# Seven blocks of the first feed-forward input and the attention's output with both operand parts in one 512-column matmul, and new tables of order

## The chip, the cores and the metric

The kernel runs on one core of one Trainium2 chip. The metric is the device time of one execution in microseconds. Five engines work side by side: TensorE (PE, with its weight loads listed as PEld), VectorE (DVE), ScalarE (ACT), GpSimd (POOL) and SyncE (SP), which here issues the transfers of weights.

## The reference, cut to what matters

Two layers at sequence 256 and width 1024, in float32. The feed-forward width is 2816, that is 22 blocks of 128.

```
mods = silu(c) @ ada_w + ada_b                   # shift, scale, gate, four sets; one more pair for kv
x = x + gate * hgrn2_mixer(modulate(x, ...))     # layer 0: gated linear recurrence
x = x + gate * swiglu(modulate(x, ...), w_in, w_out)
x = x + gate * nsa_mixer(modulate(x, ...), w_q, w_out, shared kv)   # layer 1: sparse attention
x = x + gate * swiglu(modulate(x, ...), w_in, w_out)
swiglu(h) = (silu(a) * b) @ w_out,  a, b = split(h @ w_in)
```

## The kernel before

**Products.** Each float32 product is made of reduced-precision parts. A weight chunk of 1 MB lands in one of four `raw` buffers; it has two halves of 128x1024, and each half is split into a high part `wh` (a cast on ACT, L321) and the rest `wl` (a subtraction on DVE, L325). The activations are split into `hh` and `hl` likewise. A narrow product, `mm3` (L535 to L537), is three matmuls of 256 columns for each 128 rows of the inner dimension (a k-step): wh with hh, wh with hl, wl with hh, all summed in one PSUM tile. A wide product, `gemm_wide` (L547, L548), lays hh and hl beside each other: one matmul of 512 columns with wh, and one of 256 with wl. The part from hl then stands in a half of its own and must be added: in a feed-forward block by a copy on ACT (L1197) and an addition on DVE (L1198).

**Stages.** In the profiled execution: start and the first projections to 62.6 us; the recurrence ("hgrn") to about 166; the first feed-forward input ("f0", blocks `ff_0` to `ff_21`; the first three are deferred, that is computed before the norm is known and scaled by it behind, L791) to 296.2; its output (`ffo`) to 358; the keys, values, queries and softmax of the attention ("nsa") to 507; the attention's output `nso`, eight halves of eight k-steps, to 533, the first block of the second feed-forward within it; the second feed-forward input ("f1") to 656 and its output to the end. All blocks of f1 but the deferred ones are wide, all else is narrow. A feed-forward block has two halves, the gate `a` and the value `b`; behind them stand the silu `fs` (ACT L469), the product `fg` (DVE L1188 in a deferred block, L1206 in a narrow one, L1200 in a wide one) and the split of it into `g` (ACT L530, DVE L531).

**Modulation.** The vectors from `c` need 1 MB chunks of `ada_w`. Some are reduced on DVE (L390, two per chunk), some on PE (`adapsg`, `adapsss`, L429).

**Order.** All weight chunks form one list, `SCHED`, which SP issues in that order through the four raw buffers; a buffer is given back when its chunk has been split or reduced. Each engine works through a fixed list of instructions. The tables `ORDER` set the order of chunks and steps: `hgrn` and `nsa` name projections and steps; `hada`, `f0` and `f1` say before which block a modulation chunk is taken. `PRI` gives offsets of priority to a scheduler that lays the steps of all engines side by side. `QACT` and `KACT` are bit masks that say for which of eight pieces of q's and kv's input ACT forms the scaled part instead of DVE. `residual` adds a finished piece of an output to x on DVE (L800), then forms the next layer's operand (L586 on ACT, L587 on DVE) and the sum of squares.

## Time and profile before

| | |
|---|---|
| time, three runs | 723.38, 720.93, 723.20 us; median 723.2 |
| profiled execution, its own time | 723.27 us |
| its span | 721.5 us, granted clock 0.998 |

By stage (us of busy time):

| stretch | length | PE | DVE | ACT |
|---|---|---|---|---|
| hgrn 62.6 to 166 | 103.4 | 102.58 | 79.78 | 76.63 |
| f0 in, narrow blocks, 187.8 to 296.2 | 108.4 | 108.40 | 98.99 | 53.60 |
| f0 out 296.2 to 358 | 61.8 | 61.80 | 50.73 | 28.11 |
| kv, q, softmax 358 to 507 | 149.0 | 146.52 | 125.10 | 94.35 |
| nso 507 to 533 | 26.0 | 26.00 | 19.31 | 15.96 |
| f1 in 533 to 656 | 123.0 | 122.78 | 100.28 | 74.23 |

A PE that reads as busy is one with a matmul in it; successive matmuls overlap, so the time that a matmul costs is read from the distance between starts. Idle time of an engine is given with what ended it, in square brackets behind a row or behind the second bar of a group.

### The profile page before, as it was taken

The page shows a single profiled execution, that of the slowest core. Times are in us where ns is not written, and L with a number is a line of the kernel's source. Part 1 is how long each engine was busy: PE and PEld are TensorE (multiplying, and loading weights), DVE is VectorE, ACT ScalarE, POOL GpSimd, SP SyncE. Part 2 cuts the span into 40 slices and gives each one's busy share as a digit, 9 for nine tenths or more (in the row PEclk, how much of TensorE's full clock was granted, in tenths as well). Part 3 has the DMA queues.
Part 4 walks back from the last instruction along what each step waited for, and adds up shares of the span by engine and source line. Part 5 has one row for each costly group of instructions (what it writes and reads, how often), then busy time and mean ns, then how long its engine had stood idle before and what let it go on. Part 6 is the DMA issues. An engine that isn't in the chain of part 4 may idle for free.

```text
span 721.5 us, 14615 instructions
## 1 busy us (share of the span) xinstructions
PE 710.4 (98%) x5843; PEld 628.2 (87%) x5843; DVE 578.9 (80%) x1177; ACT 418.5 (58%) x825; POOL 12.3 (2%) x29
## 2 busy tenths in 40 slices
PE   8999999999999999999999999999999999999998
PEld 5999788899999999988898896555999888888887
DVE  6997896589998989889598798878779878776651
ACT  5659877567636454544376555559657656564430
POOL 0000000000000000000002020100000000000000
PEclk9999999999999999999999999999999999999999
DMA  9899865734599898888548542674445757556720
GB/s 356 334 367 381 334 255 194 269 126 175 179 343 369 315 347 341 318 304 341 198 148 289 207 151 70 248 281 187 176 175 177 256 204 258 202 197 232 241 81 23
DMA packets 27926, 174.05 MB, mean 241 GB/s; under 512 B 3281, under 2 KB 4689, under 8 KB 8018
## 3 DMA queue, kind: packets, MB, share of 16 engines
q1 hardware_dynamic: 26656, 170.80, 64.3%
q0 software_dynamic: 768, 1.57, 0.8%
q8 instruction: 46, 0.75, 0.4%
q10 hardware_dynamic: 434, 0.74, 0.3%
q14 instruction: 22, 0.18, 0.1%
HBM read 170.48 MB, written 1.05 MB: 238 GB/s over the span
## 4 chain that ended last, share of the span: by engine, by line
PE 80%; DVE 7%; ACT 6%; DMA 4%; issue 2%; SPq 0%; ACTq 0%; DVEq 0%
PE ffo L547 11%; PE ff L535 7%; PE ff L537 7%; PE ff L536 6%; PE ffo L548 5%; PE ff L547 5%; DMA raw<-in_w 3%; PE ff L548 2%; PE po L1616 2%; PE adapsss L429 2%; DVE wl L325 2%; ACT wh L321 2%; PE ptt L1598 2%; PE s L1558 2%; ACT Pt L469 1%
## 5 line engine op out<-in xcount | busy, mean ns | idle before, releaser
L321 ACT CAST wh<-raw 128x1024 fp32r<-128x1024 f32 x199 | 206.8, 1049 | 164.0 <-PE ffo L547 43.8
L325 DVE TENSOR_TENSOR wl<-raw,wh 128x1024 fp32r<-128x1024 f32 x199 | 241.2, 1220 | 71.0 <-ACT wh L321 70.9
L547 PE MATMUL ffo<-g,wh 128*128 128x512 f32 x330 | 116.0, 394 | 0.0
L536 PE MATMUL ff<-hl,wh 128*128 128x256 f32 (+1 forms) x352 | 99.1, 282 | 0.0
L537 PE MATMUL ff<-hh,wl 128*128 128x256 f32 (+1 forms) x352 | 99.1, 282 | 0.0
L535 PE MATMUL ff<-hh,wh 128*128 128x256 f32 (+1 forms) x352 | 98.9, 282 | 0.0
L548 PE MATMUL ffo<-g,wl 128*128 128x256 f32 x330 | 93.0, 282 | 0.0
L390 DVE CUSTOM_DVE_ANT_0 junk<-raw,crep 128x1024 f32<-128x1024 f32 x64 | 77.9, 1217 | 3.1 <-DMA raw<-in_w 3.1
L547 PEld LDWEIGHTS ffo<-g,wh 128*128 128x128 f32 x330 | 62.0, 188 | 14.5
L535 PEld LDWEIGHTS ff<-hh,wh 128*128 128x128 f32 x352 | 66.3, 189 | 0.3 <-ACT hh L586 0.2
L537 PEld LDWEIGHTS ff<-hh,wl 128*128 128x128 f32 x352 | 66.5, 189 | 0.0
L536 PEld LDWEIGHTS ff<-hl,wh 128*128 128x128 f32 x352 | 66.4, 189 | 0.0
L548 PEld LDWEIGHTS ffo<-g,wl 128*128 128x128 f32 x330 | 62.0, 188 | 0.0
L547 PE MATMUL ff<-h,wh 128*128 128x512 f32 x152 | 54.1, 394 | 0.0
L548 PE MATMUL ff<-h,wl 128*128 128x256 f32 x152 | 42.6, 281 | 0.0
L469 ACT ACTIVATE Pt<-Pt,nm 128x128 f32<-128x128 f32 x64 | 28.1, 441 | 16.9 <-DVE nm L1567 16.9
L547 PEld LDWEIGHTS ff<-h,wh 128*128 128x128 f32 x152 | 28.7, 189 | 6.6
L548 PEld LDWEIGHTS ff<-h,wl 128*128 128x128 f32 x152 | 28.7, 189 | 0.0
L800 DVE SCALAR_TENSOR_TENSOR x<-ffo,mod,x 128x256 f32<-128x256 f32 x31 | 14.9, 481 | 16.5 <-PE ffo L548 11.5
L530 ACT CAST g<-fg 128x256 fp32r<-128x256 f32 x44 | 17.8, 404 | 17.4 <-DVE fg L1206 16.3
L1563 DVE CUSTOM_DVE_ANT_0 Pt<-s,cst 128x128 f32<-128x128 f32 (+1 forms) x64 | 18.9, 352 | 2.1 <-PE s L1558 2.0
L1042 DVE TENSOR_TENSOR rf<-rf 128x512 f32<-128x512 f32 x28 | 18.3, 685 | 2.2 <-ACT X L1039 1.0
(497 smaller groups left out, 1755.3 us busy)
## 6 DMA issues: line engine op xcount, KB each, us to landing
raw<-in_w SPq DMA_DIRECT2D x153, 1024.0 KB, 5.5
raw<-in_w SPq DMA_DIRECT2D x11, 512.0 KB, 6.9
w1late<-in_w SPq DMA_DIRECT2D x2, 1024.0 KB, 8.7
x<-in_x SPq DMA_DIRECT2D x2, 512.0 KB, 4.7
usq<-huq POOLq DMA_DIRECT2D x16, 64.0 KB, 2.9
out<-x SPq DMA_DIRECT2D x8, 128.0 KB, 1.9
cst<-in_cst ACTq DMA_DIRECT2D x1, 558.0 KB
usk<-huk POOLq DMA_DIRECT2D x8, 64.0 KB, 5.8
```

The costliest lines, as they stand in the source:

```text
L321: r = nc.scalar.copy(wh, u)
L325: r = nc.vector.tensor_tensor(wl, u, wh.bitcast(F32), op=ALU.subtract)
L390: r = nc.vector.tensor_tensor_reduce(out=junk, in0=t[:, h * D:(h + 1) * D], in1=self.crep, scale=1.0, scalar=0.0, op0=ALU.mult, op1=ALU.ad ...
L469: r = nc.scalar.activation(out, in_, func, **kw)
L530: self.nc.scalar.copy(hi, v)
L535: mm(ps, lhsT=wh, rhs=hh, start=first, stop=False)
L536: mm(ps, lhsT=wh, rhs=hl, start=False, stop=False)
L537: return mm(ps, lhsT=wl, rhs=hh, start=False, stop=last)
L547: mm(ps, lhsT=w[k][0], rhs=b, start=k == 0, stop=False)
L548: mm(ps[:, 0], lhsT=w[k][1], rhs=b[:, 0], start=False, stop=k == n - 1)
L1042: nc.vector.tensor_tensor(fr, fr, ap(rf, 2 * W, [1, 2], [2, n], [0, b]), op=ALU.mult)
L1563: nc.vector.tensor_tensor_reduce(out=Pt[half][:, br, o:o + n], in0=ps[half][:, br], in1=cs[:, S - n:], scale=1.0, scalar=-3e38, op0=ALU.ad ...
```

## The change

Blocks 4, 11, 14, 16, 17, 18 and 21 of f0 become wide; for that the operand `h1` is one tile with both parts beside each other. Each half of `nso` becomes wide with a PSUM tile of its own, and `residual` adds its two parts to x with two L800 in place of one. No chunk is added or taken away. The tables of order get other entries (of `hgrn` and `f0` the diff shows the lines; `hada`, `nsa` and `f1` change likewise), so do PRI and the two masks. PTV leaves the choice of engine in its line as it was. Many lines have a number higher by one in the changed kernel.

```diff
-WIDE = (1,)
+WIDE = ((4, 11, 14, 16, 17, 18, 21), range(NF))
-QACT, KACT = 0x0F, 0xF0
+QACT, KACT = 89, 241
+PTV = 1
-PRI = {"gates": -100, "av": 10, "res": 60, "rot": -15, "fh": 60}
+PRI = {'gates': -80, 'av': 10, 'res': 50, 'rot': 0, 'fh': 130}
     "hgrn": (
-        "D0 k i0 +g0 +i1 +g1 S0/4 x c0 c1 D1 i2 +i3 V0 +g2 +T0 S1/4 +g3 x G0 V1 T1 o0 H o1 G1 o2 o3"
+        "i0 k +i1 +g0 D0 +g1 S0/4 c0 x i2 c1 V0 +g2 +i3 +T0 D1 S1/4 +g3 x H G0 V1 o0 T1 G1 o1 o2 o3"
-    "f0": [7, 7, 8, 8, 9, 13, 15, 16, 16, 16, 21, 21, 22, 23, 25, 26, 28, 29, 31, 32],
+    "f0": [5, 6, 7, 8, 9, 10, 12, 13, 15, 19, 20, 20, 22, 23, 26, 26, 26, 27, 30, 32],
...
-        hh = self.hp.tile([P, KD, 258], F32R, tag=f"hh{which}", name=f"hh{which}")
-        hl = self.hp.tile([P, KD, 258], F32R, tag=f"hl{which}", name=f"hl{which}")
-        return hh, hl
+        self.h1 = self.hp.tile([P, 2, KD, 258], F32R, tag="h1", name="h1").rearrange("p e k s -> p k e s")
+        return self.h1[:, :, 0], self.h1[:, :, 1]
...
-                elif l in WIDE:
+                elif j in WIDE[l]:
+                    both = (self.h1, self.h0)[l]
...
-                        self.gemm_wide(ps[m], self.tiles(ws[m]), lambda k: self.h0[:, k, :, :S])
+                        self.gemm_wide(ps[m], self.tiles(ws[m]), lambda k: both[:, k, :, :S])
...
-                ps = self.acc_tile(f"nso{i}")
                 for m in range(2):
-                    self.gemm(ps[:, m], self.tiles(ws[m]), self.O[0], self.O[1])
-                    self.residual(ps[:, m], 2 * i + m, gate, nxt)
+                    ps = self.acc_tile(f"nso{i}_{m}")
+                    self.gemm_wide(ps, self.tiles(ws[m]), lambda k: self.h0[:, k, :, :S])
+                    self.residual(ps[:, 0], 2 * i + m, gate, nxt, ps[:, 1])
...
-                if half == 0 and br == 0:
+                if PTV >> (2 * br + half) & 1:
```

PE loses 176 matmuls, one for each wide k-step: 7 blocks of 16, and 64 in nso. Three places show the new order.

DVE at the end of the deferred blocks of f0. Before (`ISA` is the reduction L390; `u<-ff_2` are the two scaled halves of block 2; `wl_0` and `wl_1` here are the weights of blocks 5, then 6):

```order
L791 TENSOR_TENSOR u<-ff_2_0_2639,rstd 128x256
L791 TENSOR_TENSOR u<-ff_2_1_2666,rstd 128x256
L325 TENSOR_TENSOR wl_0_2698<-raw_2445,wh_0_2697 128x1024
L1188 SCALAR_TENSOR_TENSOR fg<-u,sw,fs 128x256
L325 TENSOR_TENSOR wl_1_2702<-raw_2445,wh_1_2701 128x1024
L531 TENSOR_TENSOR g<-fg,g 128x256
L1206 TENSOR_TENSOR fg<-ff_3_2709,fs 128x256
L325 TENSOR_TENSOR wl_0_2763<-raw_2455,wh_0_2762 128x1024
L531 TENSOR_TENSOR g<-fg,g 128x256
L325 TENSOR_TENSOR wl_1_2767<-raw_2455,wh_1_2766 128x1024
L1206 TENSOR_TENSOR fg<-ff_4_2774,fs 128x256
L390 ISA junk,mod_1940<-raw_2561,crep 128x1024
```

The same engine and place in the changed kernel; the wl here are those of block 5:

```order
L791 TENSOR_TENSOR u<-ff_2_0_2635,rstd 128x256
L791 TENSOR_TENSOR u<-ff_2_1_2662,rstd 128x256
L391 ISA junk,mod_2054<-raw_2442,crep 128x1024
L391 ISA mod_2054 128x1
L1188 SCALAR_TENSOR_TENSOR fg<-u,sw,fs 128x256
L391 ISA junk,mod_2054<-raw_2442,crep 128x1024
L391 ISA mod_2054 128x1
L532 TENSOR_TENSOR g<-fg,g 128x256
L414 TENSOR_TENSOR mod_2054<-mod_2054,cols 128x2
L326 TENSOR_TENSOR wl_0_2701<-raw_2452,wh_0_2700 128x1024
L326 TENSOR_TENSOR wl_1_2705<-raw_2452,wh_1_2704 128x1024
L1207 TENSOR_TENSOR fg<-ff_3_2712,fs 128x256
```

A modulation chunk (two ISA with their accumulator reads and L414) now stands between block 2 and the weights of block 5, and in the same way one before each of blocks 6 to 10; before, the first came after the weights of block 6.

PE at the end of nso. Before (`ff_0_0` and `ff_0_1` are the two halves of f1's block 0):

```order
L537 MATMUL ff_0_0_6796<-hh_6428,wl_0_6662 128x258
L535 MATMUL ff_0_0_6796<-hh_6428,wh_0_6661 128x258
L536 MATMUL ff_0_0_6796<-hl_6429,wh_0_6661 128x258
L537 MATMUL ff_0_0_6796<-hh_6428,wl_0_6662 128x258
L535 MATMUL ff_0_1_6823<-hh_6428,wh_1_6665 128x258
L536 MATMUL ff_0_1_6823<-hl_6429,wh_1_6665 128x258
L537 MATMUL ff_0_1_6823<-hh_6428,wl_1_6666 128x258
L535 MATMUL nso_6671<-h_5782,wh_1_6592 128x256
L536 MATMUL nso_6671<-h_5782,wh_1_6592 128x256
L537 MATMUL nso_6671<-h_5782,wl_1_6593 128x256
L535 MATMUL nso_6671<-h_5782,wh_1_6592 128x256
```

After:

```order
L548 MATMUL nso_1_6581<-h_5707,wh_1_6490 128x512
L549 MATMUL nso_1_6581<-h_5707,wl_1_6491 128x256
L548 MATMUL nso_1_6581<-h_5707,wh_1_6490 128x512
L549 MATMUL nso_1_6581<-h_5707,wl_1_6491 128x256
L548 MATMUL nso_1_6581<-h_5707,wh_1_6490 128x512
L549 MATMUL nso_1_6581<-h_5707,wl_1_6491 128x256
L536 MATMUL ff_0_0_6668<-h_6353,wh_0_6546 128x258
L537 MATMUL ff_0_0_6668<-h_6353,wh_0_6546 128x258
L538 MATMUL ff_0_0_6668<-h_6353,wl_0_6547 128x258
L536 MATMUL ff_0_0_6668<-h_6353,wh_0_6546 128x258
```

The last piece of nso stood behind 21 matmuls of ff_0; now nso is finished first, in pairs of 512 and 256 columns, and ff_0 follows in one piece.

DVE in the recurrence, where the decays (`rf`, L1029 to L1044) begin. Before (`wl_0_871` belongs to the projection hg_g):

```order
L1029 TENSOR_TENSOR rf_770<-rf_770,q 128x512
L1029 TENSOR_TENSOR rf_778<-rf_778,q 128x512
L1042 TENSOR_TENSOR rf_770<-rf_770 128x2x256
L1042 TENSOR_TENSOR rf_778<-rf_778 128x2x256
L1044 TENSOR_TENSOR rf_770<-rf_770 128x256
L1044 TENSOR_TENSOR rf_778<-rf_778 128x256
L1042 TENSOR_TENSOR rf_770<-rf_770 128x2x128x2
L1042 TENSOR_TENSOR rf_778<-rf_778 128x2x128x2
L1044 TENSOR_TENSOR rf_770<-rf_770 128x128
L1044 TENSOR_TENSOR rf_778<-rf_778 128x128
L325 TENSOR_TENSOR wl_0_871<-raw_704,wh_0_870 128x1024
```

After (`wl_0_821` and `wl_1_825` are both halves of the second hg_i, which now comes next on PE):

```order
L1029 TENSOR_TENSOR rf_768<-rf_768,q 128x512
L1029 TENSOR_TENSOR rf_776<-rf_776,q 128x512
L326 TENSOR_TENSOR wl_0_821<-raw_765,wh_0_820 128x1024
L326 TENSOR_TENSOR wl_1_825<-raw_765,wh_1_824 128x1024
L1042 TENSOR_TENSOR rf_768<-rf_768 128x2x256
L1042 TENSOR_TENSOR rf_776<-rf_776 128x2x256
L1044 TENSOR_TENSOR rf_768<-rf_768 128x256
L1044 TENSOR_TENSOR rf_776<-rf_776 128x256
L1042 TENSOR_TENSOR rf_768<-rf_768 128x2x128x2
L1042 TENSOR_TENSOR rf_776<-rf_776 128x2x128x2
L1044 TENSOR_TENSOR rf_768<-rf_768 128x128
```

The two subtractions for the projection that PE takes next have moved ahead of the first decay level.

## Rows read from the trace of the kernel before

**Rows 1.** The page: busy time of each engine with its share of the span and instructions; and shares of the chain that ended last.

```profile
PE 710.4 (98%) x5843; PEld 628.2 (87%) x5843; DVE 578.9 (80%) x1177; ACT 418.5 (58%) x825; POOL 12.3 (2%) x29
...
PE 80%; DVE 7%; ACT 6%; DMA 4%; issue 2%; SPq 0%; ACTq 0%; DVEq 0%
```

**Rows 2.** Busy time by stretch. Columns: stretch, its length, then PE, PEld, DVE, ACT, POOL with counts, granted clock, DMA share, GB/s.

```profile
187.80:296.20 108.40, 108.40 (x915) 108.40 (x914) 98.99 (x174) 53.60 (x81) 0.00 (x0) 1.00 0.86 325
358.00:507.00 149.00, 146.52 (x1132) 112.53 (x1131) 125.10 (x362) 94.35 (x270) 12.05 (x25) 0.99 0.56 197
507.00:533.00 26.00, 26.00 (x214) 25.51 (x213) 19.31 (x34) 15.96 (x26) 0.00 (x0) 1.00 0.53 193
```

**Rows 3.** Timeline of PE in block 5 of f0 (narrow). Columns here and in all timelines: start, duration, engine, line, operation.

```profile
205.30 0.28 PE L535 MATMUL ff<-hh,wh 128*128 128x256 f32 x1
...
207.43 0.28 PE L535 MATMUL ff<-hh,wh 128*128 128x256 f32 x1
```

**Rows 4.** Timeline of PE in block 12 of f1 (wide): the second half's first k-step, and the start of the next block.

```profile
602.90 0.39 PE L547 MATMUL ff_12b<-h,wh 128*128 128x512 f32 x1
603.13 0.28 PE L548 MATMUL ff_12b<-h,wl 128*128 128x256 f32 x1
...
605.68 0.40 PE L547 MATMUL ff<-h,wh 128*128 128x512 f32 x1
```

**Rows 5.** The page's costliest groups: count, then busy us and mean ns of one.

```profile
L547 PE MATMUL ff<-h,wh 128*128 128x512 f32 x152 | 54.1, 394 | 0.0
L548 PE MATMUL ff<-h,wl 128*128 128x256 f32 x152 | 42.6, 281 | 0.0
```

**Rows 6.** Timeline of ACT at the ends of blocks 4 and 5 of f0: the silu `fs` that waits for the end of each, and a cast that waited for its chunk.

```profile
199.50 0.38 ACT L469 ACTIVATE fs<-ff 128x256 f32<-128x256 f32 x1 [1.65 <-PE ff L537]
...
201.68 2.00 ACT L321 CAST wh<-raw 128x1024 fp32r<-128x1024 f32 x2 [0.90 <-DMA raw<-in_w]
205.20 0.39 ACT L469 ACTIVATE fs<-ff 128x256 f32<-128x256 f32 x1 [1.52 <-PE ff L537]
```

**Rows 7.** Timeline of DVE in blocks 3 to 5 of f0.

```profile
193.20 0.75 DVE L791 TENSOR_TENSOR u<-ff,rstd 128x256 f32<-128x256 f32 x2
...
195.11 0.48 DVE L1188 SCALAR_TENSOR_TENSOR fg<-u,sw,fs 128x256 f32<-128x256 f32 x1
195.51 1.22 DVE L325 TENSOR_TENSOR wl<-raw,wh 128x1024 fp32r<-128x1024 f32 x1
196.65 0.42 DVE L531 TENSOR_TENSOR g<-fg,g 128x256 fp32r<-128x256 f32 x1
196.99 0.42 DVE L1206 TENSOR_TENSOR fg<-ff,fs 128x256 f32<-128x256 f32 x1
...
200.26 1.21 DVE L390 CUSTOM_DVE_ANT_0 junk<-raw,crep 128x1024 f32<-128x1024 f32 x1
...
201.40 0.42 DVE L531 TENSOR_TENSOR g<-fg,g 128x256 fp32r<-128x256 f32 x1
...
204.02 0.15 DVE L413 TENSOR_TENSOR mod<-mod,cols 128x2 f32<-128x2 f32 x1
```

**Rows 8.** Timeline of DVE in f1: the two additions of a wide block.

```profile
558.75 0.41 DVE L1198 TENSOR_TENSOR u<-ff,u 128x256 f32<-128x256 f32 x1
559.08 0.41 DVE L1198 TENSOR_TENSOR u<-ff_3b,u 128x256 f32<-128x256 f32 x1
```

**Rows 9.** Groups of DVE in the stretch 507 to 533 (nso): the addition to x.

```profile
L800 DVE SCALAR_TENSOR_TENSOR x<-nso,mod,x 128x256 f32<-128x256 f32 x7 | 3.4, 481 | 3.5 <-PE nso L537 3.5
```

**Rows 10.** Timeline of DVE in the recurrence.

```profile
69.00 1.30 DVE L1042 TENSOR_TENSOR rf<-rf 128x512 f32<-128x512 f32 x2 [0.62 <-ACT q L1036]
...
72.53 1.21 DVE L325 TENSOR_TENSOR wl<-raw,wh 128x1024 fp32r<-128x1024 f32 x1
```

**Rows 11.** Timeline of PE at the same place.

```profile
73.80 0.39 PE L537 MATMUL hg_g<-h,wl 128*128 128x256 f32 x1 [0.63 <-DVE wl L325]
```

**Rows 12.** Timeline of DVE in the kv stage, ahead of the first weights of the attention's gates.

```profile
385.70 0.74 DVE L762 TENSOR_SCALAR t<-xr,modAkv,modkv 128x256 f32<-128x256 f32 x2
...
387.01 1.22 DVE L325 TENSOR_TENSOR wl<-raw,wh 128x1024 fp32r<-128x1024 f32 x1
```

**Rows 13.** The chain that ended last, in order of time: the transfer that follows.

```profile
388.30 9.40 DMA raw<-in_w
```

**Rows 14.** Timeline of ACT: the cast that waited for it.

```profile
397.71 1.05 ACT L321 CAST wh<-raw 128x1024 fp32r<-128x1024 f32 x1 [5.81 <-DMA raw<-in_w]
```

**Rows 15.** Timeline of PE behind that cast.

```profile
399.12 0.39 PE L988 MATMUL v<-wh,h 128*128 128x256 f32 x1 [0.43 <-ACT h L530]
...
400.74 0.39 PE L990 MATMUL v<-wh,h 128*128 128x256 f32 x1 [1.00 <-DVE h L531]
...
401.08 0.41 PE L989 MATMUL v<-wl,h 128*128 128x256 f32 x1
...
404.28 0.38 PE L535 MATMUL nq<-hh,wh 128*128 128x256 f32 x1
```

**Rows 16.** Two stretches, that of the transfer and 1 us behind PE's waits; columns as in Rows 2.

```profile
388.30:397.70 9.40, 9.40 (x85) 8.65 (x84) 5.36 (x9) 3.21 (x5) 0.00 (x0) 1.00 1.00 371
402.00:403.00 1.00, 1.00 (x6) 1.00 (x6) 1.00 (x1) 0.13 (x1) 0.00 (x0) 0.50 0.86 360
```

**Rows 17.** What PE waited for from 405 to 507 us, the longest: total, times, longest.

```profile
PE ptt L1598 <- ACT hsqq L1246: 0.2, 1, 0.2
```

More of the change, by code (lines that the diff above doesn't have):

```diff
@@ L65 @@
     "hgrn": (
-        "D0 k i0 +g0 +i1 +g1 S0/4 x c0 c1 D1 i2 +i3 V0 +g2 +T0 S1/4 +g3 x G0 V1 T1 o0 H o1 G1 o2 o3"
+        "i0 k +i1 +g0 D0 +g1 S0/4 c0 x i2 c1 V0 +g2 +i3 +T0 D1 S1/4 +g3 x H G0 V1 o0 T1 G1 o1 o2 o3"
     ).split(),
-    "hada": [1, 1, 2, 2, 3, 3, 4, 4, 7, 7, 8, 8],
-    "f0": [7, 7, 8, 8, 9, 13, 15, 16, 16, 16, 21, 21, 22, 23, 25, 26, 28, 29, 31, 32],
+    "hada": [1, 1, 1, 2, 3, 3, 4, 6, 7, 7, 9, 9],
+    "f0": [5, 6, 7, 8, 9, 10, 12, 13, 15, 19, 20, 20, 22, 23, 26, 26, 26, 27, 30, 32],
     "nsa": (
-        "K q0 c0 c1 G w0 q1 R n0 x0 q3 w1 s0 s1 s2 q2 v0 v1 n1 a s3 a s4 v2 a v3 a x1 s5 s6 v4 v6 s7 a a a a v5 a v7 a a a"
+        "q0 K c1 c0 G w0 q1 R n0 q3 q2 x0 s0 w1 s1 s2 v0 v1 n1 s3 s4 v2 a a v3 a a x1 s5 a s6 v4 v6 s7 v5 a a v7 a a a a a"
     ).split(),
-    "f1": [15, 16, 24, 29],
+    "f1": [10, 20, 21, 32],
 }
@@ L651, in startup @@
         x, v = self.x, nc.vector
-        sq = self.hp.tile([P, KD * 258], F32, tag="hh1", name="sqs")[:, :KD * S].rearrange("p (k s) -> p k s", k=KD)
+        two = self.hp.tile([P, 2, KD, 258], F32, tag="h1", name="sqs_xr0")
+        sq, self.xr0 = two[:, 0, :, :S], two[:, 1, :, :S]
         mean = self.tp.tile([P, 2, P], F32, tag="dg", bufs=1, name="mean")[:, 0]
@@ L710, in first_stat @@
         self.first_order = on_act + [A, sh], on_dve
-        self.xr0 = self.hp.tile([P, KD * 258], F32, tag="hl1", name="xr0")[:, :KD * S].rearrange("p (k s) -> p k s", k=KD)
     def stat_end(self, ps=None):
@@ L846, in hgrn @@
             v = [gp.tile([P, 2, 512], F32, tag=f"v{i}", name=f"v{i}") for i in range(2)]
-            s0 = self.hp.tile([P, KD * 258], F32, tag="hh1", name="s0")
-            s1 = self.hp.tile([P, KD * 258], F32, tag="hl1", name="s1")
+            two = self.hp.tile([P, 2, KD * 258], F32, tag="h1", name="s01")
+            s0, s1 = two[:, 0], two[:, 1]
             graw = s0[:, 1024:2048].rearrange("p (n m s) -> p n m s", n=2, m=2)
```

## The prediction

> **What bounds the kernel now.** I read the page first. PE is busy 98% of the span and holds 80% of the chain that ended last, DVE 7%, DMA 4% [rows 1]. Then the busy time by stretch: in the narrow blocks of f0 PE is busy for all of 108.40 us, in nso for all of 26.00; only the kv, query and softmax stretch leaves it 149.00 − 146.52 = 2.48 us idle [rows 2]. So a change gains in two ways: fewer or shorter PE steps, or one of the few waits of PE. The share of DVE matters too: 98.99 of 108.40 us in f0 leaves it 9.4 us, and all its work there feeds PE.
>
> The third view is the timeline of PE. Durations mislead here. By the groups a 512-column matmul lasts 394 ns and a 256-column one 281 [rows 5], so three narrow ones would be 843 ns, a wide pair 675, and a k-step would save 168. But they overlap, and the distance of starts is the price. Narrow: 205.30 to 207.43 is six k-steps, 0.355 us each, 2.84 for a half of eight; the block, from one silu's end of wait to the next, 199.50 to 205.20, is 5.70, or 2.85 a half [rows 3, 6]. Wide: 602.90 to 605.68 is a half of eight, 2.78 us [rows 4]. A half saves 0.06 to 0.07 us, not 1.3.
>
> **The change part by part.**
>
> *Wide products.* Seven blocks are 14 halves, nso is 8: 22 halves by 0.06 to 0.07 is 1.3 to 1.5 us, all on PE in stretches where it never waits. I take **−1.4**: 0.9 in f0, 0.5 in nso.
>
> The start of the 256-column matmul stands 0.23 us behind that of the 512-column one (602.90, 603.13) [rows 4]. The Trainium skill (TensorE: Matmul & The Clock Gate, Back-to-back issue gap) gives N/2.4 GHz plus about 2.5 ns from start to start, which is 216 ns for 512 columns and 109 for 256. By that rule a wide pair saves one time 2.5 ns per k-step, an estimate of 176 × 2.5 ns = 0.4 us in place of 1.4. The rows are slower than the rule for both, and they decide the sum.
>
> *What the wide blocks cost elsewhere.* Two additions on DVE per block, 0.33 us from start to start [rows 8], 0.7 a block, 4.6 to 4.9 us for seven. The idle 9.4 us of DVE in f0 [rows 2] shrink to 4.5 to 4.8, so on the whole there is cover; whether there is at each place, the next paragraph counts. In nso a second addition to x per half, 0.48 us by [rows 9], 8 × 0.48 = 3.8, in 26.00 − 19.31 = 6.7 us of idle DVE [rows 2]. PE does not wait for the pieces of nso until block 0 of f1 needs them: behind the last matmul of nso stand all the ff_0 matmuls, and the next norm's product comes after 34 of them, some 4 us at 0.12 us each, against about 2.1 us of DVE and ACT work behind the last half (two additions, an operand's two parts, a sum). Price 0; without that cover up to 2 us.
>
> *Modulation chunks earlier in f0.* This is where DVE has least to spare. The instructions of the deferred blocks ahead of the shown rows of the order are the same in both kernels but for their sequence, so the second `u<-ff_2` ends where it does now, at 193.20 + 0.67 = 193.87 [rows 7] (start to start a pair takes some 0.08 less than its 0.75). From there the new order has a reduction (1.14, from 200.26 to 201.40), fg (0.40), a reduction (1.14), g (0.34), the addition of L413 (at most 0.15) and wl of block 5 (1.14, from 195.51 to 196.65) [rows 7]: 193.87 + 4.31 = 198.2. Block 5 starts on PE at about 199.2 (the silu of block 4 starts at 199.50, when that block's last matmul, 0.28 long, has ended [rows 3, 6]), and 0.1 sooner with block 4 wide. Lead: 0.9 to 1.0 us, where the same subtraction is now done before the fg of 195.11 [rows 7], some 4.1 ahead. Carried on by the same prices (1.14 wl, 1.14 reduction, 0.34 fg, 0.34 g), block 6 has 1.4 us and block 7, behind the additions of block 4, about 1.0; blocks 8 to 10 gain 0.3 each, because DVE then needs 5.4 us a block and PE 5.70. Later blocks have more. Price **0**, with 1 us to spare; what it costs when that is used up is the second rival.
>
> *Recurrence.* PE waits 0.63 us for wl of hg_g at 73.80 [rows 11]. DVE does that subtraction at 72.53, behind two levels of decays that began at 69.00 [rows 10]. In the new order PE takes hg_i there and DVE does both its subtractions ahead of the decays, 69.00 + 1.14 = 70.1, over 2 us before PE asks. The following weights come two levels later, but PE then has a block of about 5.7 us to do. **−0.6**, between 0 (another wait of the same size behind the decays, which end 2.3 us later) and −0.63.
>
> *kv stage.* PE waits 0.43 us for h at 399.12 and 1.00 at 400.74 [rows 15]. The cause lies before: ACT's cast waited 5.81 us for its chunk [rows 14], whose transfer was issued at 388.30 and took 9.40 us [rows 13], and the h that PE needs are queued behind that cast and its subtraction. The buffer was given back by the wl of 387.01. In the new order two products L762 and one L1258 no longer stand ahead of it, as much as lies between 385.70 and 387.01 [rows 12], so the issue can come 1.3 us sooner. The DMA engines are full while it is under way (share 1.00 from 388.30 to 397.70) [rows 16], so the landing moves less than the issue. Between 0 and −1.3; I take **−0.5**, nearer to 0 because of the full queues.
>
> *Order of the queries and the softmax.* q3 and q2 now come before the first scores. The trace has only one wait left that this could remove, 0.2 us for the squares of q [rows 17], and of the 2.48 us idle of the stretch 1.43 is the kv wait; the rest, 1.05, is the most that can be had. The bound above is a new wait of the size of the largest here, 1.00 [rows 15]. I take **−0.5**, halfway to the bound: the squares leave the softmax's ACT, but no longer wait of PE goes.
>
> *The rest* (hada, f1, PRI, masks): the f1 positions fall where DVE has 123.0 − 100.28 us, as the table of stages shows. Price 0.
>
> **Sum**, against the profiled execution's own 723.27 us, which lies 0.07 above the median of the runs: −1.4 − 0.6 − 0.5 − 0.5 = −3.0, **720.3 us**. With every term at its best end it would be −1.5 − 0.63 − 1.3 − 1.05 = −4.5, 718.8; with every one at its worst, −1.3 + 1.0 = −0.3, 723.0.
>
> **The rivals.**
>
> *The clock comes back.* After those two waits the granted clock is 0.50, the 1.2 GHz level, for over 3 us [rows 16]; from 401.08 to 404.28 fifteen matmuls are 0.213 us apart and not 0.119 [rows 3, 15], which costs 1.4 us. If the chunk lands early enough for the waits to go, the clock need not fall, and 1.43 + 1.4 replace the 0.5: 723.27 − 1.4 − 0.6 − 0.5 − 2.8 = **718.0**. For it speaks that one early run of before lies at 720.93, 2.3 us under the median, which could be such a run; against it that the DMA is full and the h keep their place behind the cast. Chance 0.25.
>
> *DVE too late in f0.* The point is a lead of 1.0 us at blocks 5 and 7. One cast there waited 0.90 us for its chunk [rows 6], once. With a chunk of modulation at each of blocks 5 to 10, a buffer is wanted back every 2.85 us and DVE has 0.3 us a block in reserve; if each of the six chunks costs such a wait, 6 × 0.90 = 5.4 us, less the 1.0 of lead, PE stands 4.4 us: 720.3 + 4.4 = **724.7**, slower than before. It overtakes the gains of 3.0 from five such waits on (4.5 less 1.0). Against it: the trace shows one such wait in that place. Chance 0.12.
>
> *The wide products give next to nothing*, as the rule on the issue gap would have it: about 1 us less gained, **721.3**. The wide blocks of f1 speak against it. Chance 0.13.
>
> *The durations are right*: 176 × 0.168 = 30 us, 693. The pitches exclude it; 0.01.
>
> **How the numbers follow.** The forecast 720.3 has 0.47, the rivals 0.25, 0.12, 0.13 and 0.01, anything else 0.02. Some 0.5% (3.6 us: under 719.6, over 726.8) is what a measurement can tell from no change. Under 719.6 lie the clock's case (0.25), the forecast with the low ends of its terms (0.12) and 693 (0.01): faster 0.38. Over 726.8 lie DVE's case with waits half as long again, and a little else: slower 0.05. The rest, 0.57, is within. The range holds 8 in 10 from the clock's case with the low ends of the others, 717.0, to the middle of DVE's case, 724.0.
>
> **What would show it.** In f0 the silu of a wide block should come 5.57 us after that of the block before it and PE should wait for no wl L325; an idle gap in front of blocks 5 to 8 that names DVE is the second rival. In the recurrence the 0.63 us at hg_g should be gone. At the kv stage the cast's wait for its chunk, PE's wait for h, and the clock in the 3 us behind decide between 720 and 718. In nso the eight halves should take 22.2 us, and rb should not wait longer than now. The prediction is wrong if a new wait of PE over 1 us appears anywhere, or if wide k-steps beside a busier DVE are further apart than 0.348 us.

## The result, and the profile after

| | median | runs | ratio to before, 95% interval |
|---|---|---|---|
| before | 721.84 us | 720.93 to 723.38, 6 runs | |
| changed | 718.12 us | 716.49 to 719.47, 6 runs | 0.9946 [0.9932, 0.9959] |
| changed, once more | 716.82 us | 715.77 to 719.15, 6 runs | 0.9939 [0.9923, 0.9954] |

The changed kernel is faster by 0.54%. In the second comparison, beside 17 other runs of before with a median of 721.40 us, it is faster by 0.61%. The profiled execution took 716.89 us. The page, as in [rows 1]:

```profile
span 715.1 us, 14307 instructions
...
PE 703.6 (98%) x5667; PEld 616.3 (86%) x5667; DVE 585.7 (82%) x1198; ACT 423.9 (59%) x840; POOL 12.3 (2%) x29
...
PE 90%; DVE 4%; DMA 2%; ACT 2%; issue 1%; POOL 0%; ACTq 0%; DVEq 0%; POOLq 0%
```

PE's share of the chain went from 80% to 90%: what ends the span is now PE's own work more than its waits. The stretches that answer to [rows 2] and [rows 16] (same columns; f0's narrow and wide blocks, two microseconds in the kv stage, in PE's wait and where the clock was 0.50 before, nso):

```profile
187.00:293.00 106.00, 106.00 (x788) 101.05 (x787) 100.56 (x183) 55.97 (x92) 0.00 (x0) 1.00 0.87 324
396.00:397.00 1.00, 0.06 (x1) 0.07 (x1) 1.00 (x4) 0.42 (x2) 0.00 (x0) 1.00 1.03 426
399.00:400.00 1.00, 1.00 (x10) 1.00 (x10) 1.00 (x2) 0.00 (x0) 0.00 (x0) 1.00 0.27 107
502.40:525.00 22.60, 22.60 (x132) 19.89 (x132) 20.85 (x38) 16.33 (x27) 0.00 (x0) 1.00 0.61 215
```

In f0 DVE is busy 100.56 of 106.00 us, so its idle time fell from 9.4 to 5.4 us (4.5 to 4.8 were forecast) and PE is still busy throughout. In nso it is 20.85 of 22.60. What PE waited for behind the start (total, times, longest):

```profile
PE v L990 <- DVE h L532: 1.0, 1, 1.0
PE hb L1298 <- ACT hry L531: 0.9, 2, 0.7
...
PE rb L728 <- DVE dg L726: 0.4, 2, 0.2
...
PE v L988 <- ACT h L531: 0.2, 1, 0.2
```

The wait of hg_g [rows 11] is gone; that of v for h [rows 15] is there with 1.0 and 0.2 in place of 1.0 and 0.4; hb, which turns the normed queries, is new with 0.9 in two waits.

The two profiled executions differ by 6.4 us, the medians by 3.7. Some of the 6.4 belongs to the executions and not to the kernels. So the lengths of the stages are put side by side, each measured on PE's timeline from the first matmul of one product to the first of the next, for all profiled executions. ("kv" runs from the first kv matmul to the first of nso, "nso+f1" from there to the first ffo of f1; f0's output is 61.72 to 61.83 us and f1's output 61.98 in all.)

| kernel | start, from q | recurrence | f0 | kv, softmax | nso+f1 |
|---|---|---|---|---|---|
| before | 48.51 | 104.03 | 129.49 | 149.09 | 148.95 |
| changed | 47.91 | 102.19 | 128.87 | 147.70 | 147.25 |
| changed, again | 47.96 | 102.23 | 128.87 | 147.41 | 147.25 |
| e1 f0 wide only | 48.59 | 103.78 | 128.85 | 148.06 | 148.95 |
| e2 nso wide only | 49.90 | 103.78 | 129.49 | 149.15 | 147.27 |
| e3 tables hgrn, hada only | 48.95 | 102.52 | 129.50 | 148.04 | 148.94 |
| e4 table nsa, masks only | 47.93 | 103.66 | 129.49 | 146.96 | 148.95 |
| e5 operand tile only | 47.90 | 103.70 | 129.47 | 149.25 | 148.98 |
| e6 changed, old offsets | 49.47 | 102.64 | 128.84 | 146.88 | 147.25 |
| e7 changed, all f0 wide | 48.85 | 102.21 | 129.15 | 145.55 | 147.26 |
| e8 changed, early blocks wide | 47.97 | 102.50 | 130.39 | 147.09 | 147.28 |
| e9 changed, old offsets, 12 wide | 48.37 | 102.92 | 128.45 | 147.95 | 147.24 |
| e10 table hgrn only | 47.96 | 104.64 | 129.51 | 147.73 | 148.94 |
| e11 changed, nso narrow | 48.72 | 102.12 | 128.87 | 146.64 | 148.15 |

f0 and nso+f1 repeat within 0.03 us where the code is the same. The start scatters by 2 us, the recurrence by some 0.4, and kv by over 1: of the six executions with the nsa order of before three have 147.73 to 148.06 us and three 149.09 to 149.25, and the latter are the three with a mean granted clock of 0.997 or 0.998.

The kv stage can be divided at one place. In all fourteen executions the same 326 matmuls stand between its first matmul and the v matmul (L990) that ends PE's wait for h, and that matmul starts 3.04 to 3.06 us after the landing of the chunk of [rows 13]. With the nsa order of before it starts 42.63 to 42.91 us into the stage, in the changed kernel 42.19 and 41.95. The rest, 804 matmuls to the first of nso, takes 106.33 or 106.34 us with the old order where the clock fell, 104.88 to 105.43 where it did not, and 105.51 and 105.46 in the changed kernel.

### The profile page after: what moved, and what is told of

It reads as the page before. It is cut to its first block, busy times and chain, and to the rows that moved or that the text cites. A ratio compares the mean times of both kernels' runs of the same rounds, so it can differ in the third digit from the quotient of the medians.

```text
span 715.1 us, 14307 instructions
## 1 busy us (share of the span) xinstructions
PE 703.6 (98%) x5667; PEld 616.3 (86%) x5667; DVE 585.7 (82%) x1198; ACT 423.9 (59%) x840; POOL 12.3 (2%) x29
## 4 chain that ended last, share of the span: by engine, by line
PE 90%; DVE 4%; DMA 2%; ACT 2%; issue 1%; POOL 0%; ACTq 0%; DVEq 0%; POOLq 0%
PE ffo L548 11%; PE ff L548 7%; PE ffo L549 5%; PE ff L537 5%; PE ff L538 5%; PE ff L536 5%; PE ff L549 3%; PE po L1617 2%; PE s L1559 2%; PE adapsss L430 2%; PE nso L548 2%; PE ptt L1599 2%; DMA raw<-in_w 1%; PE hg_g L536 1%; PE hg_i L988 1%; PE adapsg L430 1%
## 5 line engine op out<-in xcount | busy, mean ns | idle before, releaser
L538 PE MATMUL ff<-h,wl 128*128 128x256 f32 (+1 forms) x288 | 81.1, 282 | 0.0
L537 PE MATMUL ff<-h,wh 128*128 128x256 f32 (+1 forms) x288 | 81.0, 282 | 0.0
L536 PE MATMUL ff<-h,wh 128*128 128x256 f32 (+1 forms) x288 | 80.9, 282 | 0.0
L548 PE MATMUL ff<-h,wh 128*128 128x512 f32 x208 | 74.0, 394 | 0.0
L549 PE MATMUL ff<-h,wl 128*128 128x256 f32 x208 | 58.4, 281 | 0.0
L538 PEld LDWEIGHTS ff<-h,wl 128*128 128x128 f32 x288 | 54.5, 189 | 0.0
L536 PEld LDWEIGHTS ff<-h,wh 128*128 128x128 f32 x288 | 54.1, 189 | 0.3
L537 PEld LDWEIGHTS ff<-h,wh 128*128 128x128 f32 x288 | 54.3, 189 | 0.0
L548 PEld LDWEIGHTS ff<-h,wh 128*128 128x128 f32 x208 | 39.2, 189 | 8.8
L549 PEld LDWEIGHTS ff<-h,wl 128*128 128x128 f32 x208 | 39.2, 188 | 0.0
L800 DVE SCALAR_TENSOR_TENSOR x<-ffo,mod,x 128x256 f32<-128x256 f32 x31 | 14.9, 482 | 16.9 <-PE ffo L549 11.9
L548 PE MATMUL nso<-h,wh 128*128 128x512 f32 x64 | 22.4, 394 | 0.0
```

The source lines that it names most:

```text
L536: mm(ps, lhsT=wh, rhs=hh, start=first, stop=False)
L537: mm(ps, lhsT=wh, rhs=hl, start=False, stop=False)
L538: return mm(ps, lhsT=wl, rhs=hh, start=False, stop=last)
L548: mm(ps, lhsT=w[k][0], rhs=b, start=k == 0, stop=False)
L549: mm(ps[:, 0], lhsT=w[k][1], rhs=b[:, 0], start=False, stop=k == n - 1)
```

## The experiments

Parts alone (e1 to e5, e10) stand on the kernel before; all of them have the one operand tile of the changed kernel, which e5 has alone. The others stand on the changed kernel. Each time is the median. The runs of before on the same chip have a median of 721.32 us for e1 to e4, 721.71 for e5 to e8 and 721.40 for e9 to e12.

**e1: seven wide blocks alone** (with the operand tile that they need).

```diff
-WIDE = (1,)
+WIDE = ((4, 11, 14, 16, 17, 18, 21), range(NF))
```

> Of the change only the seven wide blocks of the first feed-forward input (with the operand as one tile for both parts); all tables of order, masks and offsets and the attention's output stay as before. Theory A (the price is the distance of starts, and each part gains in its own place): f0 shorter by 0.6 to 0.9 us, no wait of PE on DVE's weights, everything else unchanged: 0.9 us under the kernel before, ratio 0.9988. Theory B (the changed kernel's gain is above all that the clock did not fall in the kv stage and that the start went better in the runs seen, not the edits): within 0.3 us of before. Theory C (wide blocks make DVE late unless the f0 table is changed too): a wait of PE on wl before some block between 12 and 19 and a time over before.

721.80 us, ratio 1.0004 [0.9995, 1.0012]. The stage is 0.64 us shorter, as theory A has it, and PE waits for no wl there; but the time shows no gain. Theory C falls. Between the stage and the time there is a gap of about 0.9 us that this run does not explain; e5 was made for it.

**e2: wide nso alone.**

```diff
-                ps = self.acc_tile(f"nso{i}")
...
-                    self.gemm(ps[:, m], self.tiles(ws[m]), self.O[0], self.O[1])
-                    self.residual(ps[:, m], 2 * i + m, gate, nxt)
+                    ps = self.acc_tile(f"nso{i}_{m}")
+                    self.gemm_wide(ps, self.tiles(ws[m]), lambda k: self.h0[:, k, :, :S])
+                    self.residual(ps[:, 0], 2 * i + m, gate, nxt, ps[:, 1])
```

> Of the change only the wide attention's output. Theory A2: the stage from the first to the last nso matmul loses 1.2 to 1.3 us, of which 0.5 is the closer k-steps and 0.8 that narrow halves have a few matmuls at 0.22 in place of 0.12 us where they begin, which a wide half has not: ratio 0.9983. Theory A as predicted: only the k-steps, 0.5 us, ratio 0.9993. Rival: the second addition to x per half makes the first block of the second feed-forward wait by 1 us or more, no gain.

720.38 us, ratio 0.9986 [0.9976, 0.9996]. nso+f1 is 1.68 us shorter, over three times what was predicted, more than theory A2 gave, and all of what the changed kernel shows there. The rival falls: the second addition to x makes nothing wait. Why it is more than the closer k-steps is e11's question.

**e3: tables hgrn and hada alone.** (The lines of hgrn are in the diff of the change.)

```diff
-    "hada": [1, 1, 2, 2, 3, 3, 4, 4, 7, 7, 8, 8],
+    "hada": [1, 1, 1, 2, 3, 3, 4, 6, 7, 7, 9, 9],
```

> Of the change only the order tables hgrn and hada. Theory A: the recurrence stretch (first hg_i matmul to first ff matmul) is 1.8 to 1.9 us shorter, 0.63 to 0.7 of it the wait of hg_g for its weights, the rest around the short matmuls of hgt and adapsss; ratio 0.9975. Theory B: only the wait, 0.6 us, ratio 0.9991, and the rest of the difference between the two profiled executions is scatter.

719.98 us, ratio 0.9979 [0.9970, 0.9987]. The stage is 102.52 us against 103.66 to 104.03 in the executions with the old tables: 1.1 to 1.5 us less. Theory A, somewhat smaller; theory B's 0.6 falls.

**e4: table nsa and the masks alone.** (The masks are in the diff of the change.)

```diff
-        "K q0 c0 c1 G w0 q1 R n0 x0 q3 w1 s0 s1 s2 q2 v0 v1 n1 a s3 a s4 v2 a v3 a x1 s5 s6 v4 v6 s7 a a a a v5 a v7 a a a"
+        "q0 K c1 c0 G w0 q1 R n0 q3 q2 x0 s0 w1 s1 s2 v0 v1 n1 s3 s4 v2 a a v3 a a x1 s5 a s6 v4 v6 s7 v5 a a v7 a a a a a"
```

> Of the change only the order table nsa and the two masks. Theory A: the cast behind the full DMA queue still waits and PE still waits 1.0 to 1.4 us for h; the stretch gains 0 to 0.5 us, and 1.4 more in those executions in which the clock does not fall behind the wait; ratio 0.998 to 1.000. Theory B (the order decides the clock): granted clock 1.00 through the 5 us behind that wait in the profile, and over 2 us gained, ratio 0.997.

720.58 us, ratio 0.9992 [0.9983, 1.0001]. The stage is 146.96 us, 0.8 to 1.1 less than in the executions of the old order in which the clock did not fall (147.73 to 148.06). That is more than theory A gave. PE still waits 1.0 us for h, but the wait ends 42.12 us into the stage in place of 42.63 to 42.91, so 0.5 to 0.8 of the gain lies ahead of its end; what is behind takes 104.84 us against 104.88 to 105.43. The clock is 1.00 here, but so it is in e1, e3 and e10 with the old order; theory B falls.

**e5: the tile alone.** No product and no table is changed.

```diff
-        hh = self.hp.tile([P, KD, 258], F32R, tag=f"hh{which}", name=f"hh{which}")
-        hl = self.hp.tile([P, KD, 258], F32R, tag=f"hl{which}", name=f"hl{which}")
-        return hh, hl
+        self.h1 = self.hp.tile([P, 2, KD, 258], F32R, tag="h1", name="h1").rearrange("p e k s -> p k e s")
+        return self.h1[:, :, 0], self.h1[:, :, 1]
```

> Nothing of the change but that the second operand is one tile for both parts, and with it the scratch of the start and of the recurrence in that tile. All orders, products and tables are those of before. Theory A (the start of the program scatters from run to run, whatever the kernel): within 0.3 us of before, ratio 0.9997 to 1.0003. Theory S (the scratch in rows of 256 with a gap of 2 slows the start, which is why the time of the wide blocks alone showed no gain although their stage was 0.64 us shorter): 0.5 to 1.0 us slower, ratio 1.0007 to 1.0014, with the start stage (first q matmul to first hg_i matmul) at 48.6 us or more.

721.94 us, ratio 0.9997 [0.9986, 1.0008], start 47.90 us. No cost of the tile is to be seen, and theory S's least cost (1.0007) is just inside the interval. The gap in e1 stays open: the start scatters by more than the 0.64 us in question, and the interval of e1 does not reach that gain.

**e6: the changed kernel with the offsets of before.**

```diff
-PRI = {'gates': -80, 'av': 10, 'res': 50, 'rot': 0, 'fh': 130}
+PRI = {"gates": -100, "av": 10, "res": 60, "rot": -15, "fh": 60}
```

> The changed kernel with the five offsets of priority of before. Theory R (the offset rot, now 0, lets the rotation of q come so late that hb waits 0.9 us in the attention stage, which the order table nsa alone did not show): hb waits 0.2 us or less, the stage from the first kv to the first nso matmul is 146.9 to 147.1 us in place of 147.7, 0.7 us under the changed kernel: ratio 0.9936. Rival: the wait comes from the modulation chunks and the f1 table, the stage stays at 147.7, ratio 0.9946; or the offset fh or res was worth more than that elsewhere and the time is over the changed kernel's.

717.57 us, ratio 0.9942 [0.9926, 0.9958]. The stage is 146.88 us, as theory R has it, and hb waits

```profile
PE hb L1298 <- ACT hry L531: 0.2, 1, 0.2
```

Theory R's numbers came out, and yet it does not hold alone: e8 and e11 carry the new offsets, hb waits 0.2 us in both, and their stages are 147.09 and 146.64. In the changed kernel, e7, e8 and e11 every engine has the same order of instructions from the first kv matmul to 2 us before nso, so the order does not make the difference. A transfer does. DVE, ahead of hb, waits for the last of four 64 KB transfers `usq`, which landed 4.66 and 4.60 us after its issue in the two executions of the changed kernel and 3.47 to 3.51 in e7, e8 and e11. The changed kernel, then e11:

```profile
420.41 0.75 DVE L1268 SCALAR_TENSOR_TENSOR usq<-usq,cols,cst 128x512 f32<-128x512 f32 x1 [1.51 <-DMA usq<-huq]
```

```profile
420.01 0.75 DVE L1268 SCALAR_TENSOR_TENSOR usq<-usq,cols,cst 128x512 f32<-128x512 f32 x1 [0.34 <-DMA usq<-huq]
```

In e4 and e6, with the old offsets, DVE waits there for less than 0.1 us at 3.8 and 4.0. The new offsets leave it less room; what the transfer's time depends on stays open. The offsets' price is not settled, and it is under what the time can show.

**e7: all 19 blocks wide.** `WIDE = (range(3, NF), range(NF))`

> The changed kernel with all 19 blocks 3 to 21 of the first feed-forward input wide in place of seven. PE alone would gain 12 x 0.11 = 1.3 us. Theory D (DVE sets the limit: 102.8 of 108.4 us busy with seven wide blocks, and each further one adds 0.68): DVE needs 111 us in a stretch that PE would do in 107.1, PE waits for wl L326 in several places, 3 to 4 us in all, and the stage from the first ff matmul to the first ffo matmul is 130 to 131.5 us against 128.87. Theory P (only the distance of starts counts, the rest is hidden): 127.6 us and 1.3 us under the changed kernel.

716.86 us, ratio 0.9935 [0.9918, 0.9953]. The stage is 129.15 us: neither theory. By f0's stretch, 187 to 294 us,

```profile
187.00:294.00 107.00, 106.50 (x604) 91.97 (x603) 104.67 (x198) 62.68 (x114) 0.00 (x0) 1.00 0.85 309
```

DVE is busy for 104.67 of 107.00 us, not for 111. From the timelines, wl of blocks 7 to 10 ends 0.3 to 0.8 us after PE's first matmul of the block, and matmuls there stand 1.3 us further apart than elsewhere; before block 7 and from 11 on the lead is 0.5 us or more, and the stage gains 1.0 for its twelve further blocks. The estimate of DVE's need was too high: it took all that DVE does in the stretch as due in it. The additions of the twelve further blocks do take 7.5 us, but DVE made 38 subtractions `wl` between block 3 and the end of f0 in place of 41; the three left out, 3.6 us, are for the next product, for which it was ahead. The ratio is the lowest here, but its interval holds the changed kernel's, and its kv stage of 145.55 us has another cause: in that execution v waited 0.3 us for h and hb 0.2, because the chunk ahead of it landed 9.2 us after its issue and not 10.3.

**e8: the seven wide blocks at 3 to 9.** `WIDE = ((3, 4, 5, 6, 7, 8, 9), range(NF))`

> The changed kernel with the seven wide blocks put at 3 to 9 in place of 4, 11, 14, 16, 17, 18 and 21. The number of matmuls and of additions is the same. Theory D2 (a lead of 1 us at blocks 5 and 7, as the prediction counted): the additions of 0.68 us a block go beyond DVE's reserve of 0.3 us a block, PE waits for wl before blocks 5 to 10, 2 to 3.5 us in all, and the stage is 131 to 132 us. Rival (the lead is more than counted, and the places do not matter): 128.9 us, no wait, the time of the changed kernel.

718.88 us, ratio 0.9959 [0.9944, 0.9974]. The stage is 130.39 us, 1.52 over the changed kernel's, at the same number of matmuls and additions. The place does matter; D2's lowest amount was 0.5 us too high. PE at the start of block 9 (`ff` is its first half, `ff_9b` its second), and DVE ahead of it:

```profile
220.50 0.39 PE L548 MATMUL ff_9b<-h,wh 128*128 128x512 f32 x1
221.09 0.38 PE L549 MATMUL ff<-h,wl 128*128 128x256 f32 x1 [0.20 <-DVE wl L326]
```

```profile
215.99 0.42 DVE L1199 TENSOR_TENSOR u<-ff,u 128x256 f32<-128x256 f32 x1
216.32 0.41 DVE L1199 TENSOR_TENSOR u<-ff_6b,u 128x256 f32<-128x256 f32 x1
216.66 1.21 DVE L391 CUSTOM_DVE_ANT_0 junk<-raw,crep 128x1024 f32<-128x1024 f32 x1
...
217.80 0.42 DVE L1201 TENSOR_TENSOR fg<-u,fs 128x256 f32<-128x256 f32 x1
218.13 1.22 DVE L391 CUSTOM_DVE_ANT_0 junk<-raw,crep 128x1024 f32<-128x1024 f32 x1
...
219.81 2.35 DVE L326 TENSOR_TENSOR wl<-raw,wh 128x1024 fp32r<-128x1024 f32 x2
```

The two additions, two reductions and the products stand ahead of the wl that begins at 219.81; PE starts the block at 220.27, takes a first matmul of the second half at 220.50, which needs no wl, and then must wait until 221.09. wl is late by 0.3 to 0.8 us at blocks 7 to 10, as in e7.

**e9: old offsets and twelve wide blocks.** `WIDE = ((4, 11, 12, 13, 14, 15, 16, 17, 18, 19, 20, 21), range(NF))` and PRI as in e6.

> The changed kernel with the offsets of priority of before and twelve wide blocks in the first feed-forward input (4 and 11 to 21), none of the five added ones where DVE's lead was under 2.9 us. Theory D2: no new wait in f0, five blocks by 0.1 us less, stage 128.3 us against 128.87; attention stage 146.9; in all 0.5 us under the run with the old offsets and 1.0 to 1.3 under the changed kernel, ratio 0.993. Rival (every further wide block brings DVE closer to the limit, as with all nineteen): f0 stage 128.9 or more, no gain over the old offsets alone.

717.32 us, ratio 0.9943 [0.9931, 0.9955]. f0 is 128.45 us, 0.42 less, as D2 has it within 0.15, with no wait. But kv is 147.95:

```profile
PE cmp L1454 <- DMA w1late<-in_w: 0.8, 1, 0.8
PE hb L1298 <- ACT hry L531: 0.5, 2, 0.3
```

PE waited 0.8 us for another transfer, and hb waits again, though the offsets are the old ones: the last `usq` took 4.68 us. The version does not beat the changed kernel by what can be measured.

**e10: table hgrn without hada.**

> Of the change only the order table hgrn; the modulation chunks of hada are taken where they were. Theory H (the table moves the projection whose weights come late, and the modulation matmuls that stood between the two hgt pieces): the recurrence stage (first hg_i matmul to first ff matmul) is 102.2 to 102.6 us as with both tables, against 103.7 to 104.0. Rival (hada is what takes the modulation matmuls away from hgt): only the wait of hg_g of 0.6 to 0.9 us goes, stage 103.0.

722.16 us, ratio 1.0008 [0.9999, 1.0017], stage 104.64 us: theory H falls, and more than the rival's part goes. The first decay product `psl` on PE here, and in e3 with both tables:

```profile
62.87 1.93 PE L430 MATMUL adapsg<-raw,c 128*32 128x256 f32 x32
...
71.19 0.55 PE L1113 MATMUL psl<-q,X 128*32 128x48 f32 x32 [1.12 <-ACT q L1036]
```

```profile
63.83 3.11 PE L430 MATMUL adapsg<-raw,c 128*32 128x256 f32 x48
...
72.14 0.55 PE L1113 MATMUL psl<-q,X 128*32 128x48 f32 x32
```

With the old hada two modulation chunks (`adapsg` x32) stand ahead of psl, and PE is there before ACT has made its input: 1.12 us of waiting in place of hg_g's. With the new hada a third chunk (x48) fills that time. The table hgrn gains only with hada.

**e11: the changed kernel with nso narrow, each half in a tile of its own.**

```diff
                     ps = self.acc_tile(f"nso{i}_{m}")
-                    self.gemm_wide(ps, self.tiles(ws[m]), lambda k: self.h0[:, k, :, :S])
-                    self.residual(ps[:, 0], 2 * i + m, gate, nxt, ps[:, 1])
+                    self.gemm(ps[:, 0], self.tiles(ws[m]), self.O[0], self.O[1])
+                    self.residual(ps[:, 0], 2 * i + m, gate, nxt)
```

> The changed kernel with the attention's output narrow again, but with a PSUM tile of its own for each half, and one addition to x. Theory N (narrow matmuls are 0.1 us late wherever a half begins, because the weight load of 0.19 us does not fit under a 256-column matmul when it has had to wait; 512 columns cover it): the seven to ten matmuls of 0.22 us at the starts of halves are still there, first nso to first ffo matmul of f1 148.3 to 148.9 us against 147.25, time 1.2 to 1.6 us over the changed kernel. Rival (they come from two halves sharing one PSUM tile, of which DVE reads one while PE writes the other): they are gone, the stage is 147.8, 0.6 us over.

717.55 us, ratio 0.9944 [0.9931, 0.9957]; nso+f1 148.15 us. Theory N falls. Before, where PE changes from one half of nso to another (DVE's addition of a finished half, then PE):

```profile
516.82 0.48 DVE L800 SCALAR_TENSOR_TENSOR x<-nso,mod,x 128x256 f32<-128x256 f32 x1
...
517.08 0.28 PE L536 MATMUL nso<-h,wh 128*128 128x256 f32 x1
517.36 0.39 PE L535 MATMUL nso<-h,wh 128*128 128x256 f32 x1
517.58 0.28 PE L536 MATMUL nso<-h,wh 128*128 128x256 f32 x1
```

and in e11 during the addition at the corresponding place:

```profile
512.27 0.48 DVE L800 SCALAR_TENSOR_TENSOR x<-nso,mod,x 128x256 f32<-128x256 f32 x1
512.33 0.28 PE L536 MATMUL nso<-h,wh 128*128 128x256 f32 x1
512.46 0.28 PE L537 MATMUL nso<-h,wh 128*128 128x256 f32 x1
```

Before, the matmul at 517.08 is followed after 0.28 us and the next after 0.22, and in between a half begins; in e11 all are 0.12 us apart, without being wide. The rival is right in that the shared tile is the cause, but what PE loses there is a wait. Four times before, a half of nso begins 0.05 to 0.06 us after the end of a DVE addition that began at 510.21, 516.82, 523.34 and 529.85: the trace has the matmul wait for that addition's semaphore, which came 0.04 to 0.05 us ahead of it. The second half of a tile thus does not start until the addition has read the first. Until then PE does 6, 11 and 16 matmuls of the next piece and, the last time, the 21 of ff_0; matmuls overlap, so the list of waits shows nothing. In e11 no matmul of nso waits for an addition, and every half runs through.

Of the fifteen matmuls of nso and f1 that stood at least 0.02 us further apart than usual before, 1.69 us in all, six are left in e11 with 0.84 and four in the changed kernel with 0.63. So of the 1.70 us, 0.80 came with one tile per half (and with ff_0 no longer cut in two by nso, which follows from it), and 0.90 with the width.

**e12: the changed kernel once more.**

> The changed kernel once more. Theory A (the start and the clock behind the kv wait scatter from run to run): the start stage differs from the 47.91 us of its first profile by 0.5 us or more while the recurrence, f0, f0's output, nso with f1 and f1's output agree within 0.3 us; ratio 0.994 to 0.996. Rival: all stages agree within 0.1 us and the times of a kernel lie in two groups for another cause.

716.82 us, ratio 0.9939 [0.9923, 0.9954]. Theory A expected another start; it is 47.96 us, as in the first profile, and all stages agree within 0.3. The start scatters between the other kernels of the table, which have the same order of instructions in it on PE, DVE and ACT; that it does so between executions of one kernel, these two do not show. Yet the twelve runs of the changed kernel lie in two groups, 715.8 to 717.1 (seven) and 719.1 to 719.5 (five). Both of its profiles are of the lower group, so what the upper one loses stays open.

## Why the prediction was right

It forecast 720.3 us, 3.0 under the profiled execution of before, and gave 717.0 to 724.0. The median is 718.12, the gain 0.54% where 0.41% was forecast, just beyond its bound of 0.5%. The base was high: 723.27 us is an execution in which the clock fell, 1.4 us over the median of the six runs of before. Of the 2.2 us between forecast and median most is the base, and 0.7 to 0.9 the gain. Point by point:

**Wide blocks in f0, −0.9: −0.62** (changed against before, the same in e1). The view was right and the size a little high. A wide k-step there is 0.351 us from start to start on average (0.233 and 0.118) and a narrow one 0.356, a gain of 0.005 to 0.006 and not of 0.007 to 0.009; the half at 602.90 [rows 4] was a shade better than the mean, and beside a busy DVE it is a little worse. The durations would have given 168 ns a k-step [rows 5]; they are off by a factor of thirty. One sign that the prediction set itself came out against it: wide k-steps in f0 are 0.351 us apart, more than the 0.348 that it named, and the blocks last 5.62 us in place of 5.57. The other, a new wait of over 1 us, did not come. The third rival, next to nothing, falls too: it allowed 0.4 us for f0 and nso together, which gave 0.62 and 1.70. (Wide products were not only in f1 before, as the section on that kernel has it: the outputs `ffo` of both feed-forwards are wide in both kernels, 330 matmuls of 512 columns on either page.)

**DVE's lead.** This is where the working can be checked step by step. Counted were leads of 0.9 to 1.0 us at block 5, 1.4 at 6 and 1.0 at 7; the trace of the changed kernel has 1.04, 1.51 and 1.17. DVE ahead of block 5, then PE at its start:

```profile
191.30 1.21 DVE L391 CUSTOM_DVE_ANT_0 junk<-raw,crep 128x1024 f32<-128x1024 f32 x1
...
192.44 0.48 DVE L1188 SCALAR_TENSOR_TENSOR fg<-u,sw,fs 128x256 f32<-128x256 f32 x1
192.84 1.22 DVE L391 CUSTOM_DVE_ANT_0 junk<-raw,crep 128x1024 f32<-128x1024 f32 x1
...
193.99 0.42 DVE L532 TENSOR_TENSOR g<-fg,g 128x256 fp32r<-128x256 f32 x1
194.32 0.15 DVE L414 TENSOR_TENSOR mod<-mod,cols 128x2 f32<-128x2 f32 x1
194.40 2.35 DVE L326 TENSOR_TENSOR wl<-raw,wh 128x1024 fp32r<-128x1024 f32 x2
```

```profile
195.96 0.40 PE L548 MATMUL ff_4b<-h,wh 128*128 128x512 f32 x1
196.19 0.28 PE L549 MATMUL ff_4b<-h,wl 128*128 128x256 f32 x1
196.31 0.39 PE L548 MATMUL ff_4b<-h,wh 128*128 128x512 f32 x1
...
196.66 0.28 PE L536 MATMUL ff<-h,wh 128*128 128x256 f32 x1
```

The first wl is done 1.14 us after 194.40, at about 195.6 (1.22 with its drain), and block 5 starts at 196.66. No wait came of it, the second rival did not happen; e7 and e8 show that its mechanism is real and lay 1 us away.

**nso, −0.5: −1.70** (e2 alone: −1.68). This step failed in size. The prediction counted only the distance within a k-step, −0.5, and took nso before to run at the pitch of f0's blocks. There the width gives somewhat more: in e11 a narrow half takes 2.86 to 2.87 us, in the changed kernel a wide one 2.79. What it left out is the wait of half a tile for the addition that reads the other half (e11). It goes with a tile per half, which the diff brings and the prediction named but gave no price; the timeline of before shows it, and it is why ff_0 stood ahead of the last piece.

**Recurrence, −0.6: −1.4 to −1.8** (e3: −1.1 to −1.5). The wait of hg_g went, as counted. The rest lies in the modulation matmuls: `adapsss` take 7.54 to 7.55 us from start to start in place of 8.34 to 8.53 there, with the same count of 64. In the new order no group of them is cut in two by an hgt, as one was before; that this is the reason was not tried apart. The prediction saw no price there. And the −0.6 needs hada, which was priced at 0 under "the rest": without it the wait only moves (e10).

**kv, −0.5: −0.57, and the clock.** PE's wait for h was 1.43 us and is 1.21. That is not the gain: PE also arrives 0.35 us earlier, so the end of the wait comes 0.57 us earlier in the stage (0.81 in the second profile). The issue of the chunk on SP, and the cast that still waited for it:

```profile
383.57 0.33 SPq L299 DMA_DIRECT2D raw<-in_w  x1
```

```profile
393.91 1.05 ACT L322 CAST wh<-raw 128x1024 fp32r<-128x1024 f32 x1 [5.59 <-DMA raw<-in_w]
```

5.59 us in place of 5.81 [rows 14]. Counted from the first kv matmul (357.98 us before, 354.75 now) the issue came at 28.82 in place of 30.32 and the landing at 39.14 in place of 39.71: 1.5 us and 0.57 earlier, the landing less than the issue, as argued. The clock stayed at 1.00 behind it (the window at 399 above, 44 us into the stage like that of [rows 16]), although the wait was there. The first rival tied the clock to the wait; that does not hold. With waits of 1.4 to 1.6 us the clock fell in before, e2 and e5, and with waits of 1.4 to 1.6 it did not in e3, e10 and e8. Among the 69 runs of before beside the experiments eleven have a mean clock of 0.998, among the twelve of the changed kernel none has, which can be chance; e2, with the old order there, has four of twelve at 0.997. The profile of before, 723.27 us, was one of the few in which it fell. What decides it stays open.

**Queries and softmax, −0.5: about 0 to +0.6.** Behind the end of the wait for h the stage takes 105.51 and 105.46 us, against 104.88 to 105.43 with the old order where the clock did not fall. This step failed. The order alone loses nothing (104.84 in e4, 104.48 to 104.52 in e7, e8 and e11), but in the changed kernel hb's waits of 0.8 to 0.9 take it back, a new wait of the kind and size that the upper bound of 1.00 allowed for. kv, queries and softmax together are 147.41 and 147.70 us against 147.73 to 148.06: 0.0 to −0.65.

**The rest, 0.** The tables f0 and f1 show no price: f0 is 128.87 us with the new table and 128.85 with the old (e1), nso+f1 147.25 and 147.27 (e2). hada has one, as told above.

**Sum.** −0.62 − 1.70, −1.4 to −1.8, 0 to −0.65 and −0.1 in f0's output make −3.8 to −4.9, for a measured −3.9 [−4.9, −3.0]. The parts alone, e1 to e4, add up to about −2.8 us by their ratios, with some 1.3 us of uncertainty, so the times bear the sum out only roughly. The forecast of −3.0 came near in part by luck: f0 and the queries were set too high by 0.3 and 0.5 to 1.1 us, nso and the recurrence too low by 1.2 and 0.8 to 1.2. The recurrence, kv and both wide products had the right sign, the queries had not.

## What to carry to other kernels

Price a matmul by the distance of starts in the very stage that is changed, not by its duration and not by another stage's pitch: nso ran 0.8 us slower than f0's rows would have it, which its own timeline showed. Two results that share a tile also share its waits: a reader of the one can hold up the writer of the other without any idle time in the list. Where PE is busy throughout, count the lead of the engine that feeds it, instruction by instruction in the new order; here that gave the leads within 0.2 us, and told before e8 ran that the same seven edits at other places would cost time (2 to 3.5 us forecast, 1.5 measured). What an earlier transfer gains is read from when the wait for it ends, not from how long the wait is, because the waiting engine may itself arrive earlier. An order table that removes a wait must be read together with the one that fills the time: alone, the wait moves to the next product.

## Not expected of the hardware

A transfer of 64 KB took 3.5 us or 4.6 to 4.7 from issue to landing at the same place of the same order, and PE's first wait of hb behind it was nothing or 0.7 us (e6). The stretch from the first q matmul to the first hg_i matmul takes 47.9 to 49.9 us in executions with the same order of instructions in it, three times the 0.64 us that f0's wide blocks gain. And PE's clock fell to 0.50 for some 3 us behind the same wait in some executions and stayed at 1.00 in others.
